# Norm factors and down-product evacuations given in parts a slot apart, and operand splits all on VectorE, in a one-layer streaming encoder

## The chip, the core and the metric

The kernel runs on one core of a Trainium2 chip. The metric is the device time of one execution in microseconds (us). TensorE (PE) multiplies matrices into PSUM, VectorE (DVE), ScalarE (ACT) and GpSimd (POOL) work element by element, and SyncE (SP) issues most of the transfers. Each engine works through its own instructions in order; an instruction that depends on another engine waits at the head of its queue, with everything behind it.

## The reference

The reference computes one inference step of a one-layer encoder for 1024 prompt frames and 8 × 16 sample frames, 1152 tokens in all. Token mixing (differential attention beside a short gated convolution) and cross-attention come first; the change touches only what follows them:

```
hf = rms_norm(x, g_ffn)
u_c, new_ffn = causal_dwconv(hf @ w_up, ffn_state, w_ffconv)   # width 3, per stream
x = x + (jax.nn.silu(u_c) * (hf @ w_gate)) @ w_down            # D_FF = 2816, D_MODEL = 1024
...
y_prompt = rms_norm(hp, g_final)
```

Everything is float32. Besides the two `y`, the keys, values and convolution states are outputs.

## The kernel before

All activations are stored transposed, model or feature index on the 128 partitions and the 1152 tokens along the row. A float32 product is made of three matmuls: each operand is split into a high part (ACT casts it, L111) and a low part (a subtraction, L112, on DVE or on POOL), and hi·hi, hi·lo and lo·hi are added up in PSUM.

The whole FFN is one function, `ffn()`, and its instructions are issued on each engine in the order in which the code is written, with no scheduler behind it. It has two stages.

**The up and gate products** are 154 *products* in the order of `seq`: for each pair of feature blocks (`s`) seven products P1 to P7 of a Winograd-style scheme on 2 × 2 blocks, where the token operands B11 to T4 are made once (`pair`, called by `tsplit`) and the weight sums S1 to S4 are made by POOL for each `s` (`ffn_sum`, L1059). A product is 24 matmuls of 288 columns (L1118). Product `n` is issued in *slot* `n`: first `read(n - 1)`, which takes the sums of the product before from PSUM (a DVE addition, L1127, or an ACT copy, L1125), then the split of the weights for product `n + 3`, then whatever the table `at[n]` holds, then the matmuls. `put(n, ...)` fills that table: the operand splits, POOL's sums, and for each pair of feature blocks `i` the convolution (`tap0` on ACT, `tap` on DVE), `silu`, `gate` and the store. Products that add to a PSUM bank whose partial sums are read on the way must come after that `read`: product 5 (P7) adds to the bank that `read(3)` reads, product 11 to the bank that `read(9)` reads, product 12 to that of `read(10)`.

For the first pair (`i` = 0) the values read from PSUM are still to be multiplied by the ratio of two norm factors (`rho`, L1132). `ones(0)` and `ones(1)` sum the squares over the partitions on PE after products 5 and 7, and `ratio1(t)`, `ratio2(t)` turn the sums of each half `t` of the tokens into the ratio: Square on ACT, two DVE operations (L1224, L1225), Ln, Exp and Square on ACT (L1226 to L1228), two DVE operations (L1234, L1235). Both halves use one scratch tile `z`.

**The down product** runs over three token ranges `c` (512, 384 and 256 columns, `LAST`). Its *steps* are for `c` = 0, 1 and for the first four output blocks of `c` = 2: one feature block times four output blocks `j`, 12 matmuls (L1399), 22 steps to a group `g`; the last four output blocks of `c` = 2 come one by one, 12 matmuls to a step, six steps to a block, the last of six matmuls. In step `i` the weights for step `i + 3` are split (`wsplit`), on four buffers, so that the ACT cast can begin when step `i - 1` has left its buffer. In the first four steps of each group the four finished output blocks of the group before are evacuated one by one: `evac` multiplies by the norm factor and adds the residual on DVE (L1359, L1360), then squares on ACT (L1363 or L226), adds the square up on POOL or DVE (L227), and multiplies by the final gain on ACT (L1366). `norm1` (L1373, step 7), `norm2` (step 9, by `rstd`, L192 to L197) and `norm3` (steps 10 to 17, L1382, and the store) finish a range.

Of the kernel before, what the change touches and what calls it, by code (L numbers as in the profile page):

```python
# [12 lines left out]
AF = mybir.ActivationFunctionType  # L13
# [4 lines left out]
D = 1024  # L18
# [33 lines left out]
class Step:  # L52
# [1008 lines left out]
    def ffn(self):  # L1061
# [97 lines left out]
        def tap0(i, m):  # L1159
            def f():  # L1160
                ss[i, m] = self.tile("xb", "xb", [T], 4)
# [26 lines left out]

        def new_u(i):
            def f():  # L1190
                for m in range(2):
# [9 lines left out]

        def tsplit(b, ks, pool=()):
            def f():
                for k in ks:
                    self.B[k][b] = self.pair("tu" if b == "T4" else "tb", "t", self.Tf[k][b], nc.gpsimd if k in pool else None,
                                             8 if b == "T4" else 24)
            return f
# [8 lines left out]

        def ratio1(t):

            def f():
                if t == 0:  # L1220
                    self.z = self.tile("tu", "z", [T])
                v, y, r = half(self.z, 0), half(self.z, 1), half(self.r, t)
                nc.scalar.activation(y, r, AF.Square)
                nc.vector.tensor_scalar(out=two(v), in0=banks(self.rps), scalar1=1.0 / D, scalar2=EPS, op0=ALU.mult, op1=ALU.add)  # L1224
                nc.vector.tensor_tensor(out=v, in0=v, in1=y, op=ALU.mult)  # L1225
                nc.scalar.activation(y, v, AF.Ln)  # L1226
                nc.scalar.activation(y, y, AF.Exp, scale=-0.5)
                nc.scalar.activation(r, y, AF.Square)  # L1228
            return f

        def ratio2(t):
            def f():
                v, y, r = half(self.z, 0), half(self.z, 1), half(self.r, t)
                nc.vector.scalar_tensor_tensor(out=v, in0=v, scalar=-0.5, in1=r, op0=ALU.mult, op1=ALU.mult)  # L1234
                nc.vector.scalar_tensor_tensor(out=r, in0=v, scalar=1.5, in1=y, op0=ALU.add, op1=ALU.mult)  # L1235
            return f
# [17 lines left out]
        put(2, tsplit("T1", (2, 3)), reopen)  # L1254
        put(3, tsplit("T3", (0, 1), (1,)))
        put(4, tsplit("T3", (2, 3), (3,)), self.tsubs[5])
        put(5, tsplit("T4", (0, 1), (1,)))
        put(6, tsplit("T4", (2, 3), (3,)))
        last = NFB // 2 - 1
        for i in range(last + 1):  # L1260
# [17 lines left out]
            else:  # L1278
                put(7, ratio1(0))
                put(8, ratio2(0), ratio1(1))  # L1280
                put(9, rho(0, 0), rho(0, 10), ratio2(1))
                put(10, rho(0, 11), rho(0, 1), streams(0, 1), tap0(0, 1))
                put(11, streams(0, 0), t1[0], tap0(0, 0))
                put(12, t1[1], t1[2], t1[3])
                put(13, silu(0, 1), t0[0], t0[1])
                put(14, t0[2], t0[3])
                put(15, silu(0, 0), gate(0, 1, 1))
                put(16, gate(0, 1, 0), store(0, 1))
                put(17, gate(0, 0, 0), gate(0, 0, 1), store(0, 0))

            for d in range(4):
                put(n + d + (1 if i else 3), sums(s + 1, d))
            if i < last:
                put(n + (3 if i else 5), load(s + 2))
                put(n + 10, load(s + 3))
                for d, m in enumerate((8, 9, 10, 13)):
                    put(n + m, sums(s + 2, d))
                put(n + 14, new_u(i + 1))

# [3 lines left out]
        steps += [(2, (j,), range(4 * u, min(4 * u + 4, NFB))) for j in range(4, KT) for u in range(6)]  # L1303
        raws, gx, graw, ys, sq = {}, {}, {}, {}, {}
        done = [0]
# [48 lines left out]

        def evac(c, j):
            a, b = LAST[c]
            n, end = b - a, b == T
            x, t = ys[c, j], self.tile("t8", "sq", [512], 2)[:, 0:n]
            nc.vector.tensor_tensor(out=t, in0=ch[c, j], in1=self.r[:, a:b], op=ALU.mult)  # L1359
            nc.vector.tensor_tensor(out=x, in0=t, in1=x, op=ALU.add)  # L1360
            if j == 0 or end and j >= KT - 2:
                sq.setdefault(c, []).append(self.tile("t8", "sum", [512], 3)[:, 0:n])
                nc.scalar.activation(sq[c][-1], x, AF.Square)  # L1363
            else:
                self.sumsq(sq[c][0], x, False, nc.vector if end else nc.gpsimd, self.tile("t8", "sq", [512], 2)[:, 0:n])
            nc.scalar.activation(x, x, AF.Identity, scale=self.g[:, 3, j:j + 1])  # L1366

# [6 lines left out]

        def norm2(c):
            a, b = LAST[c]
            y, v, r = (self.tile("t8", "nt", [512], 3)[:, 0:b - a] for _ in range(3))
            self.rstd(r, ch.pop(c), 1.0 / D, b - a, y, v)
            sq[c] = r

# [20 lines left out]

        new_u(0)()
        split(0)
# [29 lines left out]
        for i, (c, js, ks) in enumerate(steps):  # L1433
# [8 lines left out]
            if i < NFB:  # L1442
                operands(min(i + 3, NFB))
            if len(js) > 1:

                if k < 4 and i >= NFB:
                    evac(*((c, k) if g else (c - 1, 4 + k)))
                if g == 0 and c and k == 9:
                    norm2(c - 1)
                if g == 0 and c and 9 < k < 18:  # L1450
                    norm3(c - 1, k - 10)
                if 18 <= k:
                    xload(c, 4 * g + k - 18)
                if g and c < 2:
                    operands(NFB * (c + 1) + k + 1, 6)
            elif k == 8:
                xload(c, js[0])
            if len(js) == 1 and js[0] == 4 and ks[0] < 16:
                evac(c, k // 4)
            step(i)  # L1460
            if g == 0 and c and len(js) > 1 and k == 7:
                norm1(c - 1)
            if len(js) == 1 and ks[-1] == NFB - 1:
                evac(c, js[0])
            if i == NFB - 1:
                for q in range(3):
                    qload(NFB + 3 + q)
        norm1(2)
        norm2(2)
        for j in (0, 6, 1, 2, 7, 3, 4, 5):  # L1470
            norm3(2, j, *((nc.gpsimd, nc.scalar) if j > 5 else ()))
# [213 lines left out]
```

## Time and profile before

| | |
|---|---|
| median of 3 runs | 1705.56 us (1703.71 to 1707.20) |
| profiled execution | 1700.45 us, span 1698.7 us |
| PE busy | 1651.9 us (97%) |
| DVE busy | 1047.9 us (62%) |
| ACT busy | 675.9 us (40%) |
| POOL busy | 395.6 us (23%) |
| FFN products 0 to 153 | about 889 to 1396 us from the span's start |
| down product | about 1396 to 1688 us |

Times in rows are from the span's start. Busy PE counts overlapping matmuls, so a stretch can look busier than it is; the count of matmuls in a stretch, beside their pace where nothing waits, tells more.

### The profile page before, as it was taken

To read this page: it belongs to the slowest core of one execution; us is meant where nothing else is said; L and a number is where in the kernel's file an instruction comes from. 1 tells how busy PE (TensorE), PEld (TensorE's weight loads), DVE (VectorE), ACT (ScalarE), POOL (GpSimd) and SP (SyncE) were. 2 spreads that over 40 slices of the span, in tenths; PEclk is the share of its full clock that TensorE was granted. 3 is DMA by queue.
4 is the path that set the end of the run, shared out by engine and by line. 5 is a ranking of instruction groups with operands and counts; after the bars stand their busy time and mean duration, and the time that the engine had idled before them with its cause. 6 is when DMAs were issued, how large, how long until landed. Compare 5 with 4: busy or idle time off the path is not lost. (4 is left out here: it accounts for less than half of the span.)

```text
span 1698.7 us, 28128 instructions
## 1 busy us (share of the span) xinstructions
PE 1651.9 (97%) x10930; PEld 1566.5 (92%) x10930; DVE 1047.9 (62%) x1718; ACT 675.9 (40%) x1373; POOL 395.6 (23%) x425
## 2 busy tenths in 40 slices
PE   8999989999999999999998999999999999999997
PEld 7999879989999999988998999999999998889987
DVE  8757544777733343466768767767766664545565
ACT  7222543555523332254235333333333334443544
POOL 3223322111112321100344332333323311100000
PEclk9999999999999999999999999999999999999998
DMA  5756877534264433551441222222122247656663
GB/s 199 266 191 205 287 248 204 167 92 152 76 262 134 144 124 137 186 211 46 131 136 49 80 79 79 79 79 67 65 67 79 65 137 224 197 167 195 186 195 106
DMA packets 106566, 246.09 MB, mean 145 GB/s; under 512 B 18112, under 2 KB 57408, under 8 KB 106432
## 3 DMA queue, kind: packets, MB, share of 16 engines
q1 hardware_dynamic: 106144, 244.03, 44.1%
q8 instruction: 86, 1.41, 0.3%
q14 instruction: 48, 0.39, 0.1%
q10 hardware_dynamic: 288, 0.26, 0.0%
HBM read 186.86 MB, written 57.39 MB: 144 GB/s over the span
## 5 line engine op out<-in xcount | busy, mean ns | idle before, releaser
L111 ACT CAST wh<-raw 128x512 fp32r<-128x512 f32 x330 | 202.0, 617 | 352.0 <-PE ch L1399 104.4
L112 DVE TENSOR_TENSOR wl<-raw,wh 128x512 fp32r<-128x512 f32 (+1 forms) x276 | 196.3, 715 | 215.7 <-ACT wh L111 215.2
L1118 PE MATMUL ch<-t,wh 128*128 128x288 f32 x1408 | 284.4, 297 | 9.2 <-DVE xb L1127 5.3
L1118 PEld LDWEIGHTS ch<-t,wh 128*128 128x128 f32 x1408 | 227.1, 189 | 10.0 <-issue 8.8
L1118 PE MATMUL ch<-b,wh 128*128 128x288 f32 x1056 | 212.9, 296 | 0.0
L1118 PE MATMUL ch<-t,wl 128*128 128x288 f32 x704 | 207.9, 295 | 0.0
L112 POOL TENSOR_TENSOR wl<-raw,wh 128x512 fp32r<-128x512 f32 x54 | 71.2, 1320 | 450.2 <-ACT wh L111 412.9
L148 PE MATMUL mm<-xh,wh 128*128 128x384 f32 x496 | 169.7, 342 | 0.9 <-DVE t L824 0.9
L1118 PEld LDWEIGHTS ch<-b,wh 128*128 128x128 f32 x1056 | 169.4, 188 | 0.2
L150 PE MATMUL mm<-xh,wl 128*128 128x384 f32 x496 | 167.9, 338 | 0.1
L149 PE MATMUL mm<-xl,wh 128*128 128x384 f32 x496 | 167.6, 338 | 0.0
L1118 PE MATMUL ch<-b,wl 128*128 128x288 f32 x528 | 155.3, 294 | 0.0
L1399 PE MATMUL ch<-t,wh 128*128 128x512 f32 (+2 forms) x576 | 146.4, 341 | 6.0 <-ACT wh L111 5.9
L1118 PEld LDWEIGHTS ch<-t,wl 128*128 128x128 f32 x704 | 133.2, 189 | 0.0
L1399 PE MATMUL ch<-b,wh 128*128 128x512 f32 (+2 forms) x480 | 119.6, 337 | 1.2 <-ACT wh L111 1.2
L1399 PEld LDWEIGHTS ch<-t,wh 128*128 128x128 f32 x576 | 102.2, 193 | 16.1 <-ACT wh L111 7.9
L1399 PE MATMUL ch<-t,wl 128*128 128x512 f32 (+2 forms) x288 | 98.5, 342 | 1.0 <-DVE wl L112 0.7
L1118 PEld LDWEIGHTS ch<-b,wl 128*128 128x128 f32 x528 | 99.4, 188 | 0.0
L148 PEld LDWEIGHTS mm<-xh,wh 128*128 128x128 f32 x496 | 93.4, 188 | 3.7 <-issue 1.6
L150 PEld LDWEIGHTS mm<-xh,wl 128*128 128x128 f32 x496 | 93.5, 188 | 0.5 <-DVE wl L112 0.4
L149 PEld LDWEIGHTS mm<-xl,wh 128*128 128x128 f32 x496 | 93.5, 188 | 0.4
L1399 PEld LDWEIGHTS ch<-b,wh 128*128 128x128 f32 x480 | 84.3, 190 | 7.8 <-ACT wh L111 1.4
(367 smaller groups left out, 3646.7 us busy)
## 6 DMA issues: line engine op xcount, KB each, us to landing
raw<-in_w_dn SPq DMA_DIRECT2D x55, 512.0 KB, 4.0
raw<-in_w_ug SPq DMA_DIRECT2D x44, 512.0 KB, 4.7
gscr<-xb SPq DMA_DIRECT2D x22, 576.0 KB, 3.2
kv<-in_kc SPq DMA_DIRECT2D x16, 512.0 KB, 5.8
kv<-in_vc SPq DMA_DIRECT2D x16, 512.0 KB, 6.1
qd<-qscr SPq DMA_DIRECT2D x64, 128.0 KB, 3.5
kv<-in_km SPq DMA_DIRECT2D x16, 512.0 KB, 6.2
kv<-in_vm SPq DMA_DIRECT2D x16, 512.0 KB, 5.8
```

The costliest lines, as they stand in the source:

```text
L111: self.nc.scalar.copy(out=h, in_=x)
L112: (eng or self.nc.vector).tensor_tensor(out=l, in0=x, in1=fl(h), op=ALU.subtract)
L148: self.nc.tensor.matmul(out, lhsT=ah, rhs=bh, start=i == 0, stop=False)
L149: self.nc.tensor.matmul(out, lhsT=ah, rhs=bl, start=False, stop=False)
L150: self.nc.tensor.matmul(out, lhsT=al, rhs=bh, start=False, stop=i == n - 1)
L1118: nc.tensor.matmul(o, lhsT=w[:, ks], rhs=y[:, ts], start=start and k == 0 and i == 0, stop=k == 3 and i == 2, skip_group_check=True)
L1399: nc.tensor.matmul(ch[c, j], lhsT=p[:, w], rhs=y, start=k == 0 and m == 0, stop=k == NFB - 1 and m == 2)
```

## The change

Three things change, all in `ffn()`; the instructions and their sizes stay the same but for the engine of some.

1. The low parts of four operand blocks (T3 and T4, blocks 1 and 3) are subtracted on DVE, no longer on POOL.
2. The norm ratio has three parts (`ratio(t, 0..2)`), each in a later slot than the one before, and each half has its own scratch: the tile that later takes the convolution (`ss`), in place of the shared `z`. The first pair's convolution, `silu`, gates and stores move one or two slots later, and one buffer of `u` is taken a slot later for it.
3. In the down product `evac` becomes `evac1` (the two DVE operations) and `evac2` (Squares, sums and gain), which the next step calls, behind its weight split. `norm2` is spread over steps 9 and 10, `norm3` over 11 to 18. For the last range the squares of blocks 1 to 3 are added on POOL, no longer on DVE.

```diff
-            def f():
-                for k in ks:
-                    self.B[k][b] = self.pair("tu" if b == "T4" else "tb", "t", self.Tf[k][b], nc.gpsimd if k in pool else None,
+                    self.B[k][b] = self.pair("tu" if b == "T4" else "tb", "t", self.Tf[k][b], None, 8 if b == "T4" else 24)
...
+        def ratio(t, part):
...
+                if part == 0:
+                    ss[0, 1 - t] = self.tile("xb", "xb", [T], 4)
+                z = ss[0, 1 - t]
+                v, y, r = half(z, 0), half(z, 1), half(self.r, t)
+                if part == 0:
+                    nc.scalar.activation(y, r, AF.Square)
+                    nc.vector.tensor_scalar(out=two(v), in0=banks(self.rps), scalar1=1.0 / D, scalar2=EPS, op0=ALU.mult, op1=ALU.add)
+                    nc.vector.tensor_tensor(out=v, in0=v, in1=y, op=ALU.mult)
+                elif part == 1:
+                    nc.scalar.activation(y, v, AF.Ln)
+                    nc.scalar.activation(y, y, AF.Exp, scale=-0.5)
+                    nc.scalar.activation(r, y, AF.Square)
+                else:
+                    nc.vector.scalar_tensor_tensor(out=v, in0=v, scalar=-0.5, in1=r, op0=ALU.mult, op1=ALU.mult)
+                    nc.vector.scalar_tensor_tensor(out=r, in0=v, scalar=1.5, in1=y, op0=ALU.add, op1=ALU.mult)
...
-                put(9, rho(0, 0), rho(0, 10), ratio2(1))
-                put(10, rho(0, 11), rho(0, 1), streams(0, 1), tap0(0, 1))
+                put(9, ratio(0, 2), rho(0, 0), rho(0, 10), ratio(1, 1))
+                put(10, ratio(1, 2), rho(0, 11))
+                put(11, rho(0, 1), streams(0, 1), tap0(0, 1))
...
+        def evac2():
+            while part:
+                c, j = part.pop()
+                x, n, end = ys[c, j], LAST[c][1] - LAST[c][0], LAST[c][1] == T
+                if j == 0 or end and j >= KT - 2:
+                    sq.setdefault(c, []).append(self.tile("t8", "sum", [512], 3)[:, 0:n])
+                    nc.scalar.activation(sq[c][-1], x, AF.Square)
+                else:
+                    self.sumsq(sq[c][0], x, False, nc.vector if end and j > 3 else nc.gpsimd, self.tile("t8", "sq", [512], 2)[:, 0:n])
+                nc.scalar.activation(x, x, AF.Identity, scale=self.g[:, 3, j:j + 1])
...
+            evac2()
             if len(js) > 1:
 
                 if k < 4 and i >= NFB:
-                    evac(*((c, k) if g else (c - 1, 4 + k)))
-                if g == 0 and c and k == 9:
-                    norm2(c - 1)
-                if g == 0 and c and 9 < k < 18:
-                    norm3(c - 1, k - 10)
+                    evac1(*((c, k) if g else (c - 1, 4 + k)))
+                if g == 0 and c:
+                    if k in (9, 10):
+                        norm2(c - 1, k == 10)
+                    if 10 < k < 19:
+                        norm3(c - 1, k - 11)
```

PE's instructions stand in the same order before and after. Three places show what moves on the others.

DVE in slots 3 and 4, before: `u` from `ch` is a read (the first row is `read(2)`, the fourth `read(3)`), `t` from `xb` the low part of an operand block, `wl` that of a weight block.

```order
L1127 TENSOR_TENSOR u_9176<-ch_9307,u_9178 128x576
L112 TENSOR_TENSOR wl_9334<-raw_9207,wh_9333 128x512
L112 TENSOR_TENSOR t_9338<-xb_8212,t_9337 128x576
L1127 TENSOR_TENSOR u_9176<-ch_9347,u_9176 128x576
L112 TENSOR_TENSOR wl_9374<-raw_9050,wh_9373 128x512
L112 TENSOR_TENSOR t_9378<-xb_8685,t_9377 128x576
L1015 TENSOR_TENSOR xb_8923<-xb_8923,xa_8922 128x576
```

The same place after the change.

```order
L1127 TENSOR_TENSOR u_9178<-ch_9307,u_9176 128x576
L112 TENSOR_TENSOR wl_9334<-raw_9207,wh_9333 128x512
L112 TENSOR_TENSOR t_9338<-xb_8212,t_9337 128x576
L112 TENSOR_TENSOR t_9342<-xb_8447,t_9341 128x576
L1127 TENSOR_TENSOR u_9178<-ch_9347,u_9178 128x576
L112 TENSOR_TENSOR wl_9374<-raw_9050,wh_9373 128x512
L112 TENSOR_TENSOR t_9378<-xb_8685,t_9377 128x576
L112 TENSOR_TENSOR t_9382<-xb_8923,t_9381 128x576
L1015 TENSOR_TENSOR xb_8923<-xb_8923,xa_8922 128x576
```

`read(3)` has one split more in front of it, and POOL's four sums for `s` = 1, which stood in turn with these splits in POOL's queue, now stand there one after another.

ACT in slots 7 to 9, before: `z` is the ratio's scratch, `c_9_84` the norm factors, the copy into `xb_9472` is `read(8)`.

```order
L111 CAST wh_9506<-raw_9209 128x512
L1223 ACTIVATE z_9510<-c_9_84 128x576
L1226 ACTIVATE z_9510<-z_9510 128x576
L1227 ACTIVATE z_9510<-z_9510 128x576
L1228 ACTIVATE c_9_84<-z_9510 128x576
L111 CAST wh_9544<-S_1705_9345 128x512
L1223 ACTIVATE z_9510<-c_9_84 128x576
L1226 ACTIVATE z_9510<-z_9510 128x576
L1227 ACTIVATE z_9510<-z_9510 128x576
L1228 ACTIVATE c_9_84<-z_9510 128x576
L1125 COPY xb_9472<-ch_9480 128x576
L111 CAST wh_9583<-S_1734_9478 128x512
```

The same place after; `xb_9510` and `xb_9548` are the two halves' scratch.

```order
L111 CAST wh_9506<-raw_9209 128x512
L1225 ACTIVATE xb_9510<-c_9_84 128x576
L111 CAST wh_9541<-S_1705_9345 128x512
L1229 ACTIVATE xb_9510<-xb_9510 128x576
L1230 ACTIVATE xb_9510<-xb_9510 128x576
L1231 ACTIVATE c_9_84<-xb_9510 128x576
L1225 ACTIVATE xb_9548<-c_9_84 128x576
L1125 COPY xb_9472<-ch_9480 128x576
L111 CAST wh_9579<-S_1734_9478 128x512
L1229 ACTIVATE xb_9548<-xb_9548 128x576
L1230 ACTIVATE xb_9548<-xb_9548 128x576
L1231 ACTIVATE c_9_84<-xb_9548 128x576
```

`read(8)` and the weight casts have moved ahead of the Ln, Exp and Square that were given a slot earlier.

ACT at the first steps of the down product's second group for `c` = 1, before: the cast of the weights (`wh`), then Square and gain of the evacuated block (`ys`).

```order
L111 CAST wh_16133<-raw_15985 128x512
L1363 ACTIVATE sum_16142<-ys_16063 128x384
L1366 ACTIVATE ys_16063<-ys_16063,c_6_79 128x384
L111 CAST b_16145<-S_2558_15559 128x256
L111 CAST wh_16165<-raw_16023 128x512
L226 ACTIVATE sq_16172<-ys_16081 128x384
```

After.

```order
L111 CAST wh_16132<-raw_15982 128x512
L111 CAST b_16141<-S_2557_15558 128x256
L111 CAST wh_16161<-raw_16020 128x512
L1370 ACTIVATE sum_16165<-ys_16062 128x384
L1373 ACTIVATE ys_16062<-ys_16062,c_6_79 128x384
L111 CAST b_16171<-S_2562_15580 128x256
```

The next step's weight cast now stands ahead of the Square, at this and the other group changes alike.

## Rows read from the trace of the kernel before

**Rows 1.** PE's waits in the down product: total us, times, longest.

```profile
PE ch L1399 <- ACT wh L111: 7.1, 7, 1.4
```

**Rows 2.** Stretches: length, PE, PEld, DVE, ACT, POOL busy (instructions), clock, DMA.

```profile
910.00:920.00 10.00, 9.16 (x64) 8.55 (x64) 8.75 (x10) 4.08 (x7) 6.00 (x5) 1.00 0.19 56
934.20:941.00 6.80, 3.81 (x16) 3.84 (x17) 6.08 (x10) 2.65 (x4) 2.63 (x5) 0.50 0.04 5
980.00:1396.00 416.00, 416.00 (x3126) 416.00 (x3125) 288.74 (x376) 147.10 (x224) 123.61 (x161) 1.00 0.23 78
1515.00:1534.00 19.00, 17.37 (x94) 15.94 (x94) 9.41 (x15) 9.58 (x16) 5.14 (x4) 1.00 0.28 89
1565.00:1582.00 17.00, 15.76 (x89) 14.87 (x87) 9.41 (x18) 9.32 (x20) 3.03 (x3) 1.00 0.36 115
1582.00:1612.00 30.00, 30.00 (x173) 30.00 (x174) 16.80 (x34) 14.82 (x33) 0.00 (x0) 1.00 0.71 216
1612.00:1629.00 17.00, 13.11 (x96) 11.88 (x96) 8.58 (x17) 8.46 (x16) 4.02 (x4) 1.00 0.34 108
1629.00:1653.00 24.00, 24.00 (x199) 23.73 (x198) 17.40 (x31) 11.15 (x20) 0.00 (x0) 1.00 0.84 276
1653.00:1663.00 10.00, 8.30 (x61) 7.60 (x59) 5.42 (x13) 5.48 (x13) 0.00 (x0) 0.91 0.37 115
1663.00:1688.00 25.00, 25.00 (x188) 24.75 (x189) 13.45 (x26) 10.95 (x22) 0.00 (x0) 0.90 0.38 112
```

**Rows 3.** PE in order of time at products 5 and 11: start, us, instruction [idle before].

```profile
908.68 0.50 PE L1118 MATMUL ch<-t,wh 128*128 128x288 f32 x2 [3.03 <-DVE u L1127]
...
937.19 0.82 PE L1118 MATMUL ch<-t,wh 128*128 128x288 f32 x2 [5.34 <-DVE xb L1127]
```

**Rows 4.** DVE in order of time, slots 2 to 4.

```profile
902.86 1.42 DVE L112 TENSOR_TENSOR t<-xa,t 128x576 fp32r<-128x576 f32 x2
...
904.86 1.26 DVE L112 TENSOR_TENSOR wl<-raw,wh 128x512 fp32r<-128x512 f32 x1
906.04 1.82 DVE L112 TENSOR_TENSOR t<-xb,t 128x576 fp32r<-128x576 f32 x1
907.79 0.75 DVE L1127 TENSOR_TENSOR u<-ch,u 128x576 f32<-128x576 f32 x1
```

**Rows 5.** POOL in order of time: a split and a sum, and a sum of a later slot.

```profile
902.79 2.78 POOL L112 TENSOR_TENSOR t<-xb,t 128x576 fp32r<-128x576 f32 x1 [8.57 <-ACT t L111]
905.54 1.71 POOL L1059 TENSOR_TENSOR S<-raw,raw 128x512 f32<-128x512 f32 x1
...
1027.54 1.29 POOL L1059 TENSOR_TENSOR S<-raw,S 128x512 f32<-128x512 f32 x1 [2.36 <-DVE wl L112]
```

**Rows 6.** ACT in order of time, the second half's ratio and what stands behind it.

```profile
927.97 0.69 ACT L1223 ACTIVATE z<-c 128x576 f32<-128x576 f32 x1 [3.25 <-DVE c L1235]
...
931.72 0.62 ACT L1125 COPY xb<-ch 128x576 f32<-128x576 f32 x1
932.24 0.62 ACT L111 CAST wh<-S 128x512 fp32r<-128x512 f32 x1
```

**Rows 7.** ACT in order of time, first evacuation of blocks 4 to 7 of `c` = 1.

```profile
1612.90 0.62 ACT L111 CAST wh<-raw 128x512 fp32r<-128x512 f32 x1 [1.15 <-PE ch L1399]
1615.39 0.52 ACT L226 ACTIVATE sq<-ys 128x384 f32<-128x384 f32 x1 [1.88 <-DVE ys L1360]
...
1616.47 0.60 ACT L111 CAST wh<-raw 128x512 fp32r<-128x512 f32 x1
```

**Rows 8.** DVE, the same evacuation.

```profile
1613.55 0.69 DVE L112 TENSOR_TENSOR wl<-raw,wh 128x512 fp32r<-128x512 f32 x1 [1.05 <-ACT wh L111]
1614.16 0.55 DVE L1359 TENSOR_TENSOR sq<-ch,c 128x384 f32<-128x384 f32 x1
1614.74 0.56 DVE L1360 TENSOR_TENSOR ys<-sq,ys 128x384 f32<-128x384 f32 x1
```

**Rows 9.** POOL, the sum of that square.

```profile
1615.99 1.01 POOL L227 TENSOR_TENSOR sum<-sum,sq 128x384 f32<-128x384 f32 x1 [35.25 <-ACT sq L226]
```

More of the change, by code (lines that the diff above doesn't have):

```diff
@@ L1187, in store, with new_u @@
             return lambda: nc.sync.dma_start(out=self.gscr[:, 2 * i + m], in_=gs[i, m])
-        def new_u(i):
+        def new_u(i, *ms):
             def f():
-                for m in range(2):
+                for m in ms:
                     us[i, m] = self.tile("u", "u", [HALO + T], 2)
@@ L1297, in ffn @@
                     put(n + m, sums(s + 2, d))
-                put(n + 14, new_u(i + 1))
+                put(n + 14, new_u(i + 1, 1))
+                put(n + 14 + (not i), new_u(i + 1, 0))
         steps = [(c, range(4 * g, 4 * g + 4), (k,)) for c in range(3) for g in range(2) for k in range(NFB) if (c, g) != (2, 1)]
@@ L1303, in ffn @@
         steps += [(2, (j,), range(4 * u, min(4 * u + 4, NFB))) for j in range(4, KT) for u in range(6)]
-        raws, gx, graw, ys, sq = {}, {}, {}, {}, {}
+        raws, gx, graw, ys, sq, part = {}, {}, {}, {}, {}, []
         done = [0]
@@ L1353, in xload, with evac1 @@
             nc.sync.dma_start(out=ys[c, j], in_=self.x2[:, j, a:b])
-        def evac(c, j):
+        def evac1(c, j):
             a, b = LAST[c]
-            n, end = b - a, b == T
-            x, t = ys[c, j], self.tile("t8", "sq", [512], 2)[:, 0:n]
+            x, t = ys[c, j], self.tile("t8", "sq", [512], 2)[:, 0:b - a]
             nc.vector.tensor_tensor(out=t, in0=ch[c, j], in1=self.r[:, a:b], op=ALU.mult)
             nc.vector.tensor_tensor(out=x, in0=t, in1=x, op=ALU.add)
[L1361 to L1366, printed above, removed]
+            part.append((c, j))
+        def evac2():
[8 more added lines that the diff above has]
+                nc.scalar.activation(x, x, AF.Identity, scale=self.g[:, 3, j:j + 1])
         def norm1(c):
@@ L1373, in norm1, with norm2 @@
                 nc.tensor.matmul(ch[c], lhsT=self.ones, rhs=z, start=i == 0, stop=i == len(sq[c]) - 1)
-        def norm2(c):
+        def norm2(c, last=False):
             a, b = LAST[c]
-            y, v, r = (self.tile("t8", "nt", [512], 3)[:, 0:b - a] for _ in range(3))
-            self.rstd(r, ch.pop(c), 1.0 / D, b - a, y, v)
-            sq[c] = r
+            if not last:
+                y, v, r = norm = [self.tile("t8", "nt", [512], 3)[:, 0:b - a] for _ in range(3)]
+                nc.scalar.activation(y, ch[c], AF.Ln, bias=self.eps, scale=1.0 / D)
+                nc.vector.tensor_scalar(out=v, in0=ch[c], scalar1=-0.5 / D, scalar2=-0.5 * EPS, op0=ALU.mult, op1=ALU.add)
+                nc.scalar.activation(y, y, AF.Exp, scale=-0.5)
+                nc.scalar.activation(r, y, AF.Square)
+                sq[c] = norm
+            else:
+                y, v, r = sq[c]
+                nc.vector.tensor_tensor(out=v, in0=v, in1=r, op=ALU.mult)
+                nc.vector.scalar_tensor_tensor(out=r, in0=v, scalar=1.5, in1=y, op0=ALU.add, op1=ALU.mult)
+                sq[c] = r
         def norm3(c, j, eng=nc.vector, q=nc.sync):
@@ L1467, in ffn @@
                     qload(NFB + 3 + q)
+        evac2()
         norm1(2)
         norm2(2)
+        norm2(2, True)
         for j in (0, 6, 1, 2, 7, 3, 4, 5):
```

54 lines of the change are left out of this document (20 added, 34 removed).

## The prediction

> **What bounds the kernel now.** I read the chain of waits on the page first: outside PE it has hardly more than ACT and DVE work at a few places, so PE sets the time and only its holes can be won. PE's stretches come next. Between 980 and 1396 us, PE is busy throughout, 416.00 us for 3126 matmuls or 0.133 us each, so a product of 24 takes 3.19 us [rows 2]. The holes stand on either side of that stretch.
>
> At the start of the FFN, PE stands still for 3.03 us before product 5, waiting for `read(3)` on DVE, and for 5.34 us before product 11, waiting for `read(9)` [rows 3]. After the second hole began, the granted clock was 0.50 in 934.2 to 941.0, the lower of its two levels (1.2 of 2.4 GHz), while after the first it stayed at 1.00 in 910 to 920 [rows 2].
>
> In the down product I count matmuls, since busy time hides short holes. Where nothing waits, a matmul of 384 columns takes 30.00/173 = 0.173 us, one of 256 columns 24.00/199 = 0.121 us. The five disturbed stretches then lose 19 − 94 × 0.1734 = 2.7, 17 − 89 × 0.1734 = 1.6, 17 − 96 × 0.1206 = 5.4, 10 − 61 × 0.1206 = 2.6 and 25 − 188 × 0.1206 = 2.3 us, together 14.6 us; the last two are partly the clock, at 0.91 and 0.90 [rows 2]. PE waits there for the weight cast on ACT, seven times, 7.1 us by its records [rows 1].
>
> **The down product, part by part.** In the evacuation steps before, ACT casts the weights at 1612.90, then stands with Square at its head until DVE has subtracted, multiplied and added, and starts Square at 1615.39; the next cast starts at 1616.47 [rows 7]. So one step lasts 1616.47 − 1612.90 = 3.57 us, though PE needs 12 × 0.121 = 1.45. DVE's share is 0.69 + 0.55 + 0.56 = 1.80 us [rows 8], ACT's own 0.62 + 0.52 and a gain that ends by the next cast (16.47 − 15.39 = 1.08 for Square and gain), 1.7 in all. Neither engine is full; the chain that runs from one to the other and back is. Four such steps fall behind by 4 × (3.57 − 1.45) = 8.5 us, and the lead of three steps (4.3 us) covers half; 4.2 of the 5.4 us are explained so.
>
> With `evac2` a step later the next cast stands ahead of Square, and DVE works on the next weights while ACT squares. A step then costs the busier engine, DVE, 1.8 us, and up to 1.0 more where POOL's sum (1.01 us [rows 9]) takes turns with it. The lag is 4 × (1.8 − 1.45) = 1.4 us, at worst 4 × (2.8 − 1.45) = 5.4. I take 1.8 with two such turns in four steps, 1.4 + 2.0 = 3.4 us, inside the lead of 4.3: no hole. For `c` = 1 the step is 12 × 0.173 = 2.08 us and the same work falls behind less; at the single blocks of `c` = 2 all operations are shorter (256 columns). The sums moved from DVE to POOL there end long before the last block, whose tail is unchanged. `norm2` in two parts and `norm3` a step later add no instruction; DVE has 0.69 + 0.56 in a 1.45 us step there, and `norm1` is in time as long as the last of four sums ends two steps after the last evacuation. SP's stores move by one step behind one more weight load, which nothing waits for. Of the 14.6 us I keep 0.4 as a rest: gain 14.2. With no hole there is nothing that I can see to drop the clock near 1661 us, so its share is in that sum.
>
> **The start of the FFN.** Three effects, in order of the slots.
>
> *Splits on DVE.* Four low parts leave POOL. Beside POOL, a DVE split took 1.82 us at 906.04 and a weight split 1.26 at 904.86, against 0.71 each for the two at 902.86, while the read at 907.79, one of whose inputs is PSUM, took its plain 0.75 [rows 4]. POOL's sum took 1.71 at 905.54 and 1.29 at 1027.54; its split of 902.79 took 2.78, about as long as the two DVE splits beside it and then itself [rows 5]. The DVE split is longer by 1.1, most of one POOL operation: the two take turns, whole instruction by whole instruction. Each added split costs DVE 0.7 and saves such a turn, about zero for DVE as a whole. But the sums of `s` = 1, so far held behind POOL's splits, now come one after another from about 902.9 on, when DVE has read the old S3. Before `read(3)`, DVE has a weight split and two operand splits, three turns at 1.29.
>
> Walk: `read(2)` ends at 904.9; without POOL, 0.6 + 2 × 0.7 bring `read(3)` to an end at 907.6. With three turns, one begun during `read(2)`, it ends at 910.5 and product 5 starts at 910.6, 1.9 us later than before. I take the turns, because the rows at 904.86 and 906.04 show one in front of each.
>
> The Trainium skill, "SBUF — State Buffer", section "Who interferes with whom", says that a DVE instruction with two SBUF inputs and a GpSimd instruction that reads SBUF exclude each other, the later one blocked to the end of the first. By that rule the four sums, now in one run, give back at the start what moving the splits saves, and the time is the one forecast here; if DVE went first, as it did at 902.86, it would be that of the first rival. The rows at 904.86 and 906.04 agree with the rule, those of 1.26 and 1.82 us against 0.71.
>
> *The clock.* Product 4 ends at 908.68 − 3.03 = 905.65, so the hole becomes 4.95 us. A hole of 5.34 us brought the clock down in this trace and one of 3.03 did not; at 4.95 I expect a fall, of the same 6.8 us at half speed, so 3.4 us lost.
>
> *The ratio.* Before, the second half's first Square waited 3.25 us for the end of the first half's ratio (the shared `z`), and `read(8)` and the next weight cast started only at 931.72 and 932.24 behind its Ln, Exp and Square [rows 6]; the ratio's end on DVE and then `read(9)`, for which PE waited, came after both. Now `read(8)` and the cast stand ahead of them, and `read(9)` stands behind the cast's low part, the first half's two last operations and two `rho`, while the second half's end comes after it.
>
> From 910.6, product 11 can start on PE after six products, two `ones` of about 0.8 and the clock loss: 910.6 + 19.2 + 1.6 + 3.4 = 934.8. On the other side, product 8 ends at 928.4, ACT copies and casts to 929.6, DVE takes one turn (1.3), the low part, four operations of 0.7 and `read(9)`, ending at about 934.8. They meet; product 11 starts at 935, product 12 at 938.1 at full clock. Before, product 11 started at 937.19 and lost 3.81/2 = 1.9 us to the half clock [rows 2], so product 12 followed at 942.3. Gain 4.2 us.
>
> The bounds: if POOL takes no turns, the hole before product 5 is 2.0 us, there is no fall, and product 11 starts when DVE is through, about 932: gain 7.2. On the other side, products 11, 12 and 17 are each met with under 0.5 us to spare by this walk, and one more turn for each costs 3 × 1.29 = 3.9: gain 0.3. The convolution, `silu` and gates, one or two slots later, come into slots where DVE has 2 to 3 us of work for 3.19 and hide there; their stores end before the buffers are taken again three slots later. If that cover were gone, one turn (1.3 us) would show.
>
> **Sum.** 14.2 + 4.2 = 18.4 us off the profiled execution, 1700.45 − 18.4 = 1682.0. That execution stood 5.1 us under the median of runs; from the median, 1705.56 − 18.4 = 1687.2.
>
> **Rivals.**
>
> *No fall of the clock* (24 in 100). For it: 3.03 us left the clock alone, and POOL may get fewer turns, as at 902.86. Against it: the turns at 904.86 and 906.04. Gain 7.2 + 14.2 = 21.4, time 1684.2.
>
> *The sums hold Square* (18). ACT's Square and DVE's product share two `sq` buffers, so a Square must wait until POOL has added the one before. A step is then 0.52 + 1.01 + a turn of up to 0.7 = 2.2 us, four fall behind by 3.1, and with the 1.4 us that a weight split takes the lead is used up; in the second half of the down product (5.4 + 2.6 + 2.3) about half stays. Against it: POOL's sum can run while DVE reads PSUM. Gain 4.2 + 14.2 − 5.2, time 1692.4.
>
> *No difference* (4). The stalls only change their names, ACT behind DVE becoming DVE behind ACT, and the start gives back 3: about 1705.
>
> *Slower* (4). POOL in front of DVE. If all seven sums of the first two sets take a turn before `read(9)`, DVE has 7 × 1.29 + 4 × 0.7 = 11.8 us more in front of it; product 5 starts at 912, 3.3 us later than before, the clock falls there (3.4 us) and again at product 11, which waits as before, and products 12 and 17 wait a turn each (2.6): 9.3 us lost. This decides once `read(9)` ends after about 940, and it makes the kernel slower only if POOL's turns also keep two thirds of the holes in the down product: +9.3 − 4.9, time 1710.
>
> My own case has 50 in 100. About 0.2%, 3.4 us, is what a measurement of this kernel tells from none: faster 0.92, same 0.04, slower 0.04. The range reaches from the second case less the noise of the runs to beyond the third, 1680 to 1697.
>
> **What would show it.** Right: in the down product no wait of PE for the weight cast near the four group changes, 0.121 us a matmul through them, Square about one step behind its addition, clock 1.00 up to the tail; at the start a hole of 4 to 5 us at product 5 ended by `read(3)`, a half-clock stretch right after it, POOL's four sums in one run beside DVE splits of 1.8 us, and no hole at product 11. Wrong: a hole before product 11 or 12 of over 1.5 us, PE waiting for a cast that waited for a Square behind POOL's sum, or the clock at half near the end of the down product without a hole.

## The result and the profile after

The changed kernel takes 1679.64 us (median of 4 runs, 1678.54 to 1682.56) where the kernel before, timed beside it, takes 1704.63 (1703.46 to 1707.20, 4 runs): a ratio of 0.9854, interval 0.9836 to 0.9872. It is faster by 25 us, not by the 18.4 forecast, and ends 0.36 us below the stated range. The profiled execution took 1678.54 us, span 1676.8, granted clock 0.994 on average. Its page begins so (share of the span, instructions):

```profile
PE 1642.3 (98%) x10930; PEld 1562.9 (93%) x10930; DVE 1052.8 (63%) x1719; ACT 677.7 (40%) x1373; POOL 390.9 (23%) x424
```

I cut each execution at three marks: the first matmul of product 0, the first of the down product, and the end of its last one.

| us from the span's start | before | after |
|---|---|---|
| product 0 begins | 889.50 | 888.94 |
| down product begins | 1396.01 | 1389.77 |
| its last matmul ends | 1687.93 | 1666.07 |
| span | 1698.7 | 1676.8 |
| products 0 to 153 | 506.51 | 500.83 |
| down product | 291.92 | 276.30 |

Between the two profiles, 5.68 us come from the start of the FFN, 15.62 from the down product and 0.56 from ahead of product 0, where nothing is changed. The tail behind the last matmul is 10.7 us in both.

**Down product.** PE's waits from product 0 on, by what it waited for (total us, times, longest). The first belongs to the start. In the down product the seven for the weight cast [rows 1] are gone; the norm's sum (L1380) is left.

```profile
PE ch L1118 <- DVE u L1127: 4.6, 1, 4.6
...
PE ch L1380 <- ACT sum L1370: 0.6, 1, 0.6
```

Stretches after, in the columns of [rows 2]. The first belongs to the start and is read below; the second is the undisturbed middle of the FFN, the others span disturbed parts of the down product.

```profile
909.80:913.20 3.40, 3.40 (x15) 3.40 (x16) 3.40 (x6) 0.00 (x0) 0.23 (x1) 0.50 0.44 116
970.00:1386.00 416.00, 416.00 (x3126) 416.00 (x3125) 288.72 (x374) 148.04 (x226) 125.81 (x164) 1.00 0.23 77
1505.00:1524.00 19.00, 19.00 (x105) 18.22 (x104) 13.60 (x19) 10.47 (x18) 5.19 (x4) 1.00 0.47 156
1602.00:1619.00 17.00, 17.00 (x141) 16.73 (x140) 12.92 (x21) 12.60 (x23) 4.07 (x4) 1.00 0.58 180
1619.00:1643.00 24.00, 24.00 (x203) 24.00 (x202) 18.75 (x35) 12.69 (x25) 2.08 (x3) 1.00 0.82 258
1643.00:1653.00 10.00, 10.00 (x86) 10.00 (x85) 6.96 (x14) 5.72 (x12) 0.15 (x1) 1.00 0.74 208
1653.00:1666.00 13.00, 13.00 (x110) 13.00 (x110) 5.67 (x11) 5.32 (x11) 0.00 (x0) 1.00 0.18 55
```

The middle is the same, 3126 matmuls in 416 us. Below it the count is the thing to read: 105 in 19 us where there were 94, and 141 in 17, 203 in 24, 86 in 10 and 110 in 13 us, 0.116 to 0.121 us each, where [rows 2] had 96 in 17 and 61 in 10.

PE's order is the same in both kernels, so each matmul can also be set beside itself. Counted from the first matmul of the stage, the kernel before falls behind by 2.6, 2.0, 5.5 and 5.6 us at the four group changes: the matmul that starts at 1628.53 before, behind the third, starts at 1612.23 after, 232.52 us into its stage against 222.46. The last of the four holds the 6.8 us at half clock from 1661.2 of the kernel before, worth at most 3.4 us; after the change the clock stays at 1.00 there.

ACT in the evacuation that answers to [rows 7]:

```profile
1603.43 0.62 ACT L111 CAST wh<-raw 128x512 fp32r<-128x512 f32 x1 [0.86 <-PE ch L1416]
1604.45 0.52 ACT L226 ACTIVATE sq<-ys 128x384 f32<-128x384 f32 x1 [0.40 <-DVE ys L1361]
1605.01 0.62 ACT L1373 ACTIVATE ys<-ys,c 128x384 f32<-128x384 f32 x1
1605.53 0.60 ACT L111 CAST wh<-raw 128x512 fp32r<-128x512 f32 x1
1606.58 0.53 ACT L226 ACTIVATE sq<-ys 128x384 f32<-128x384 f32 x1 [0.45 <-DVE ys L1361]
```

From cast to cast it is 1605.53 − 1603.43 = 2.10 us, before 3.57. Square still starts right behind its own addition (1603.80 + 0.56 = 1604.36, Square at 1604.45) and waits 0.40 us for it. But the block it squares is that of the step before the cast at 1603.43, so no chain runs any more from one cast through DVE's addition and Square to the next cast, and DVE goes from one step to the next without a pause. Its addition takes 0.56 us in the first step, as in [rows 8], and 1.02 in the next, where POOL's sum runs beside it from 1605.05 and lasts as long: the two take turns (DVE's rows, then POOL's).

```profile
1603.80 0.56 DVE L1361 TENSOR_TENSOR ys<-sq,ys 128x384 f32<-128x384 f32 x1
1604.27 0.69 DVE L112 TENSOR_TENSOR wl<-raw,wh 128x512 fp32r<-128x512 f32 x1
1604.88 0.55 DVE L1360 TENSOR_TENSOR sq<-ch,c 128x384 f32<-128x384 f32 x1
1605.46 1.02 DVE L1361 TENSOR_TENSOR ys<-sq,ys 128x384 f32<-128x384 f32 x1
1606.41 0.68 DVE L112 TENSOR_TENSOR wl<-raw,wh 128x512 fp32r<-128x512 f32 x1
...
1636.83 0.43 DVE L1361 TENSOR_TENSOR ys<-sq,ys 128x256 f32<-128x256 f32 x1 [0.84 <-DMA ys<-x]
```

```profile
1605.05 1.02 POOL L227 TENSOR_TENSOR sum<-sum,sq 128x384 f32<-128x384 f32 x1 [38.01 <-ACT sq L226]
```

Four such steps fall behind by 4 × (2.10 − 1.45) = 2.6 us, inside the lead of 4.3. DVE also waits for the residual's transfer now (0.84 us at 1636.83), which PE does not feel.

**Start of the FFN.** PE's answer to [rows 3], then DVE and POOL in the place of [rows 4, 5].

```profile
909.72 0.75 PE L1118 MATMUL ch<-t,wh 128*128 128x288 f32 x2 [4.63 <-DVE u L1127]
```

```profile
904.31 1.12 DVE L112 TENSOR_TENSOR wl<-raw,wh 128x512 fp32r<-128x512 f32 x1
905.35 3.55 DVE L112 TENSOR_TENSOR t<-xb,t 128x576 fp32r<-128x576 f32 x2
908.83 0.74 DVE L1127 TENSOR_TENSOR u<-ch,u 128x576 f32<-128x576 f32 x1
...
931.45 0.75 DVE L1127 TENSOR_TENSOR xb<-ch,xb 128x576 f32<-128x576 f32 x1
```

```profile
902.47 2.41 POOL L1059 TENSOR_TENSOR S<-raw,raw 128x512 f32<-128x512 f32 x1 [7.83 <-DVE wl L112]
904.96 1.60 POOL L1059 TENSOR_TENSOR raw<-raw 128x512 f32<-128x512 f32 x1
906.63 1.66 POOL L1059 TENSOR_TENSOR S<-raw,raw 128x512 f32<-128x512 f32 x1
908.37 1.66 POOL L1059 TENSOR_TENSOR S<-raw,S 128x512 f32<-128x512 f32 x1
```

POOL's four sums stand in one run; beside them two DVE splits take 3.55 us (1.42 where DVE had the way, [rows 4]), `read(3)` ends at 909.6, and the hole before product 5 grows from 3.03 to 4.63 us. The clock falls in the stretch from 909.80, but that lasts 3.40 us. After it PE shows no wait: `read(9)` is through at 932.2, product 11 starts at 932.39 with no hole before it, and product 12 at 935.86. ACT has `read(8)` and the weight cast ahead of the ratio's second part, where they stood behind it until 931.72 [rows 6]:

```profile
926.19 0.64 ACT L1125 COPY xb<-ch 128x576 f32<-128x576 f32 x1 [1.07 <-PE ch L1118]
926.73 0.62 ACT L111 CAST wh<-S 128x512 fp32r<-128x512 f32 x1
927.25 0.69 ACT L1229 ACTIVATE xb<-xb 128x576 f32<-128x576 f32 x1
```

### The profile page after: what moved, and what is told of

Its sections match the earlier page's. It is cut to its first block, busy times and chain, and to the rows that moved or that the text cites. A ratio compares the mean times of both kernels' runs of the same rounds, so it can differ in the third digit from the quotient of the medians.

```text
span 1676.8 us, 28132 instructions
## 1 busy us (share of the span) xinstructions
PE 1642.3 (98%) x10930; PEld 1562.9 (93%) x10930; DVE 1052.8 (63%) x1719; ACT 677.7 (40%) x1373; POOL 390.9 (23%) x424
## 4 chain that ended last, share of the span: by engine, by line
PE 88%; DVE 6%; ACT 3%; DMA 2%; issue 1%; POOL 0%; DVEq 0%; SPq 0%; ACTq 0%; POOLq 0%
PE ch L1118 29%; PE ch L1416 16%; PE mm L148 8%; PE mm L150 8%; PE mm L149 8%; PE tr L148 3%; PE tr L149 3%; PE tr L150 3%; PE tr L655 2%; PE sc L616 1%; PE tr L642 1%; PE sc L523 0%; DVE t L112 0%; PE mm L817 0%; DVE p L631 0%
## 5 line engine op out<-in xcount | busy, mean ns | idle before, releaser
L1118 PEld LDWEIGHTS ch<-b,wh 128*128 128x128 f32 x1056 | 169.4, 188 | 0.5 <-issue 0.3
L1059 POOL TENSOR_TENSOR S<-raw,raw 128x512 f32<-128x512 f32 x44 | 73.5, 1670 | 81.0 <-DVE wl L112 78.4
```

Of the source, the lines that this page charges most:

```text
L1059: self.nc.gpsimd.tensor_tensor(out=w[o], in0=w[x], in1=w[y], op=op)
L1118: nc.tensor.matmul(o, lhsT=w[:, ks], rhs=y[:, ts], start=start and k == 0 and i == 0, stop=k == 3 and i == 2, skip_group_check=True)
```

## The experiments

The theory: the down product's gain comes from `evac2` running a step later, the start's gain from the ratio given in parts, and the splits on DVE are worth about nothing, since they trade POOL's splits for POOL's sums in the turns. Rivals: that the splits carry part of the gain; that the last range's sums on POOL or the spread norm, not the step later, mend the evacuation; that the whole difference includes a drift of the runs. A kernel's ratio below is to the kernel before in the same session, the stages are those of the table.

| | ratio (interval) | products 0–153 | down product |
|---|---|---|---|
| down part alone | 0.9905 (0.9892–0.9918) | 506.68 | 276.30 |
| start alone | 0.9979 (0.9970–0.9988) | 500.84 | 294.03 |
| `evac2` in the same step | 0.9977 (0.9968–0.9987) | 500.66 | 293.89 |
| before, itself | 1.0001 (0.9991–1.0012) | 506.75 | 292.08 |
| splits alone | 1.0004 (0.9995–1.0013) | 508.69 | 292.10 |
| ratio alone | 0.9969 (0.9956–0.9981) | 500.24 | 293.89 |
| sums of `s` = 1 on DVE | 0.9866 (0.9851–0.9880) | 498.71 | 276.30 |
| after, itself | 0.9880 (0.9864–0.9895) | 500.84 | 276.30 |
| all but the splits | 0.9866 (0.9831–0.9901) | 500.22 | 276.30 |
| `read(3)` first | 0.9860 (0.9831–0.9889) | 499.14 | 276.30 |

### The two halves apart

The kernel before with the down product's hunks of the change alone, and with the hunks of the start alone:

```diff
+            evac2()
             if len(js) > 1:
...
-                    evac(*((c, k) if g else (c - 1, 4 + k)))
+                    evac1(*((c, k) if g else (c - 1, 4 + k)))
```

> Only the down product's part of the change (evacuation in two parts a step apart, the last norm in parts). Theory A, the two halves of the change are independent and each hole is the chain between ACT and DVE: the down product takes 276.3 us from its first to its last matmul as in the changed kernel (291.9 before), the FFN products keep their 506.5 us; time about 1704.6 - 15.6 = 1689, or down to 1685 if other executions lose more to the clock than the profiled one. Rival, the down product's gain came from the clock or the transfers being moved by the earlier part: less than 10 us of gain here.

> Only the FFN's start (operand splits on DVE, norm ratio in three parts, convolution one or two slots later). Theory A: the FFN products take 500.8 us (506.5 before), the down product keeps 291.9; time about 1704.6 - 5.7 = 1699, or 1697 if one more fall of the clock goes. Rival, the parts depend on each other: the gains of this and of the down product alone do not add up to the 25.0 us between the medians by more than 4 us.

The down part alone takes 1686.38 us beside 1702.17 and has the down product of the changed kernel to the hundredth, 276.30. Its PE waits at the FFN's start are the old ones:

```profile
PE ch L1118 <- DVE xb L1127: 5.3, 1, 5.3
PE ch L1118 <- DVE u L1127: 3.0, 1, 3.0
```

The start alone takes 1698.88, with the products' 500.84. So each part alone gives its own stage the changed kernel's time. The test of the expectation, whole gains that add up to 25.0 us within 4, is missed all the same: 15.8 + 3.3 = 19.1. The 25.0 was itself high, a later session has 19.9 for the changed kernel; and the start alone loses some of its gain again, since its down product, whose code is that of before, takes 294.03 instead of 291.92. The waits are the same seven of 7.1 us; what differs is the clock. Here is the start alone in two stretches of the down product:

```profile
1620.30:1627.10 6.80, 5.70 (x22) 4.58 (x21) 3.22 (x6) 3.83 (x7) 0.99 (x1) 0.50 0.45 136
1657.90:1664.70 6.80, 6.32 (x29) 5.79 (x28) 4.54 (x9) 4.06 (x9) 0.00 (x0) 0.50 0.31 83
```

Of the six profiles that have the holes, three had one such fall (1661.2 in the kernel before) and three had two; the six without the holes had none. All three with two have the ratio in parts, and so reach the down product some 6 us sooner; why that matters stays open. The price is the 2 us by which the stage differs.

### The evacuation in one step

The changed kernel, with `evac2` called where `evac1` ends:

```diff
             part.append((c, j))
+            evac2()
```

> The changed kernel with one thing put back: the second part of each evacuation (Square, sum, gain) is called in the same step as the first, ahead of the next weight cast. Theory A, the order of cast and Square on ACT makes the holes: they come back at the four group changes, a step of 4.05 us at 512 columns and 3.56 at 384, down product about 290 us, time about 1679.6 + 14 = 1694 or more. Rival B, the move of the last sums from DVE to POOL and of the norm's parts made the gain: holes stay away at the first three changes and the time stays within 4 us of 1679.6.

The old holes are back, 6.8 us in seven waits, and the down product takes 293.89. ACT stands with Square at the head of its queue for 2.15 us, and 4.05 us lie from cast to cast:

```profile
1520.00 0.61 ACT L111 CAST wh<-raw 128x512 fp32r<-128x512 f32 x1
1522.76 0.63 ACT L226 ACTIVATE sq<-ys 128x512 f32<-128x512 f32 x1 [2.15 <-DVE ys L1361]
1523.42 0.73 ACT L1374 ACTIVATE ys<-ys,c 128x512 f32<-128x512 f32 x1
1524.05 0.60 ACT L111 CAST wh<-raw 128x512 fp32r<-128x512 f32 x1
```

The time is 1698.99 us (about 290 and 1694 were expected). This kernel has the sums on POOL, the spread norm and everything else of the change, and by themselves they gain nothing in the down product: without the step later nothing is left of its gain. That the stage is 2 us longer than before goes with a second fall of the clock, near 1621, as in the start alone. Whether the step later would do as well without the spread norm was not run.

### The kernel before, against itself

> The kernel before itself, for the spread of its executions: the profiled one took 1700.5 us where the runs took 1703.5 to 1707.2. Theory C, the difference is the clock, each hole lets it fall in some executions and not in others: executions of about 1704 show a mean granted clock below the 0.991 of the profiled one, by about 3 to 4 us / 1700 times two, so 0.986 to 0.988, and a profile has one more half-clock stretch. Rival, the difference has nothing to do with the clock: the granted clock is 0.991 in the longer executions too.

It came out at 1702.68 (1699.43 to 1706.57, 12 runs), ratio 1.0001; its profiled run took 1704.06, its clock 0.989, where 0.986 to 0.988 was expected; over the twelve runs the clock goes from 0.992 in the shortest to 0.988 and 0.989 in the two longest. The stages from product 0 on repeat to 0.2 us, but product 0 begins at 892.69, 3.2 us later than in the profile that the prediction went by. Over all profiles it begins between 888.94 and 893.15, whatever the kernel. One place where this arises is near 40 us: this profile of the kernel before, and then the one that the prediction went by.

```profile
40.20:47.00 6.80, 6.63 (x18) 5.54 (x19) 5.87 (x12) 1.66 (x4) 3.32 (x5) 0.50 0.55 163
```

```profile
40.20:47.00 6.80, 6.80 (x39) 6.30 (x38) 6.54 (x13) 1.67 (x4) 4.04 (x5) 1.00 0.60 183
```

It has 18 matmuls in the stretch against 39: the clock is at its lower level in one execution of the same code and not in the other. The kernel before has medians of 1704.63, 1702.17, 1701.98 and 1702.17 in the four sessions, the three later ones each on another chip, so the 1705.56 of three runs lay about 3 us above what it usually takes.

### The start, taken apart

The four splits on DVE and nothing else; and the ratio in parts with its moved slots and nothing else:

```diff
-        put(3, tsplit("T3", (0, 1), (1,)))
+        put(3, tsplit("T3", (0, 1)))
...
```

```diff
...
-                put(8, ratio2(0), ratio1(1))
-                put(9, rho(0, 0), rho(0, 10), ratio2(1))
+                put(8, ratio(0, 1), ratio(1, 0))
+                put(9, ratio(0, 2), rho(0, 0), rho(0, 10), ratio(1, 1))
...
```

> Only the four operand splits moved from POOL to DVE, all else as before. Theory D, the splits give nothing by themselves, since POOL's sums then run beside DVE in one go: product 5 waits 4.6 us and the clock falls as in the changed kernel, product 11 still waits over 4 us; FFN products 506.5 to 509 us, time within 3 us of the kernel before. Rival, taking POOL off DVE's port is itself the gain: the hole before product 11 shrinks by more than 2 us and the FFN products take under 504.5 us.

> Only the norm ratio in three parts with two scratch tiles and the convolution later; the four splits stay on POOL. Theory D, this part makes the whole gain at the start: hole of 3.0 us before product 5 without a fall of the clock, no hole over 1 us before product 11, FFN products 499 to 501 us. Rival, the ratio needs DVE free of POOL's splits: a hole of over 2 us stays before product 11 and the FFN products take more than 502.5 us.

The splits alone make the products 2.2 us longer (508.69 against 506.51): the hole at product 5 grows to 4.63 us, the clock falls there, and product 11 still waits.

```profile
913.87 0.82 PE L1118 MATMUL ch<-t,wh 128*128 128x288 f32 x2 [4.63 <-DVE u L1127]
...
942.71 0.82 PE L1118 MATMUL ch<-t,wh 128*128 128x288 f32 x2 [4.87 <-DVE xb L1127]
```

In the whole time that does not show (1.0004). The ratio alone gives the start's gain in full, 500.24. It keeps the hole of 3.04 us before product 5:

```profile
909.39 0.50 PE L1118 MATMUL ch<-t,wh 128*128 128x288 f32 x2 [3.04 <-DVE u L1127]
```

Yet the clock fell for 3.40 us from 910.2 in this one, behind a hole no longer than that of [rows 3], behind which it had not fallen; no fall was expected here.

### POOL's sums taken out of the way

The changed kernel with the sums of `s` = 1 on DVE:

```diff
-        self.nc.gpsimd.tensor_tensor(out=w[o], in0=w[x], in1=w[y], op=op)
+        (self.nc.vector if s == 1 else self.nc.gpsimd).tensor_tensor(out=w[o], in0=w[x], in1=w[y], op=op)
```

> The changed kernel with the four weight sums of s = 1 on DVE too, so that POOL is idle in slots 3 to 6. Theory E, a POOL sum beside DVE costs DVE a turn of up to 1.3 us and on DVE 0.6: read(3) ends by 907.8 (in the changed kernel's time), the hole before product 5 shrinks to 2 to 3 us and the clock doesn't fall, but product 11 is bound by DVE, so the FFN products gain 0.3 to 2 us of 500.8 only. Rival 1, the hole before product 5 is itself the price: they gain 3.5 us or more. Rival 2, DVE and POOL share the port by turns of less than an instruction and POOL's help was real: read(3) ends no earlier and the products take 1 us or more longer.

> The changed kernel itself beside the kernel before on one chip. Theory C, the spread of both kernels lies in the first 50 us, which the change doesn't touch: its executions spread over about 4 us, the longer ones with a half-clock stretch near 40 us and the first FFN product 2 to 3 us later; the FFN products take 500.8 and the down product 276.3 us whatever the total is; ratio to the kernel before 0.986 to 0.988. Rival, the spread belongs to the FFN's holes: the stages from product 0 on vary by 2 us or more from one profile to the other.

DVE now carries four additions more and is through earlier all the same, since the splits are back at 1.42 us a pair:

```profile
906.53 0.68 DVE L112 TENSOR_TENSOR wl<-raw,wh 128x512 fp32r<-128x512 f32 x1
907.13 1.42 DVE L112 TENSOR_TENSOR t<-xb,t 128x576 fp32r<-128x576 f32 x2
908.47 0.69 DVE L1059 TENSOR_TENSOR S<-raw,raw 128x512 f32<-128x512 f32 x1
909.07 0.75 DVE L1127 TENSOR_TENSOR u<-ch,u 128x576 f32<-128x576 f32 x1
```

Product 0 begins at 891.16 in this trace and at 888.94 in that of the changed kernel; counted from there, `read(3)` ends 18.66 us on against 20.63, 2.0 us earlier. The hole before product 5 is 2.65 us, the products take 498.71, 2.1 less than the changed kernel's 500.84 beside it. So the turns are real and worth about 2 us. The Trainium skill, "SBUF — State Buffer", section "Who interferes with whom", has a DVE instruction with two SBUF inputs and a GpSimd one that reads SBUF exclude each other to the end of the first; 3.55 us beside the sums against 1.42 without them agree. The clock fell all the same, for 3.40 us at 909.4, so the shorter hole did not save it, against the expectation. The changed kernel itself repeats its stages, 500.84 and 276.30, and begins product 0 at 892.42, 3.5 us later than in its first profile. In whole times the two cannot be told apart well: 1678.56 (1677.64 to 1683.03) and 1682.04 (1679.40 to 1685.33), the intervals of the ratios overlapping.

### Without the splits, and with the read first

The changed kernel with the four splits back on POOL; and the kernel with the sums of `s` = 1 on DVE, but with `read(3)` ahead of the later splits and of the sums:

```diff
...
-        put(3, tsplit("T3", (0, 1)))
+        put(3, tsplit("T3", (0, 1), (1,)))
...
```

```diff
...
-                put(n + d + (1 if i else 3), sums(s + 1, d))
+                put(n + d + 1 if i else (4, 5, 5, 8)[d], sums(s + 1, d))
...
+            if n == 3:
+                pass
+            elif n == 4:
+                tsplit("T3", (2, 3))()
+                split(6)
+                split(7)
...
```

> The changed kernel with the four operand splits back on POOL; ratio and down product as changed. Theory D, the splits on DVE are no gain in this change: FFN products 500.2 us as with the ratio alone (500.8 in the changed kernel), hole of 3.0 us before product 5, down product 276.3; time the same as the changed kernel within 2 us, 0.6 us less by the stages. Rival, the parts only work together: the products take over 502.5 us, or the down product over 278.

> The changed kernel with the four weight sums of s = 1 on DVE (as in the run with the sums on DVE) and, in slots 3 and 4, read(3) and the T3 splits ahead of the weight splits 6 and 7 and of the first sum. Theory F, DVE's queue in front of read(3) is all that holds product 5, so read(3) ends 1.2 us earlier by the two instructions of 0.6 us that now stand behind it: hole before product 5 of 1.3 to 1.6 us (2.65 with the sums alone), no fall of the clock there (worth 1.7 us), and FFN products 495.5 to 497.5 us (498.7 with the sums alone); time 1.5 to 3 us under that. Rival, DVE's work as a whole up to read(9) sets product 11: a hole of 1 to 3 us opens before product 11 or 12 and the products stay within 0.7 us of 498.7.

Without the splits the products take 500.22, 0.6 us less than with them, and no fall of the clock follows product 5. That is as much as the ratio alone (500.24), which has the same code in this stage and had the fall: here PE gets ahead and waits for operand splits instead:

```profile
912.33 0.50 PE L1118 MATMUL ch<-t,wh 128*128 128x288 f32 x2 [3.04 <-DVE u L1127]
915.15 0.40 PE L1118 MATMUL ch<-t,wh 128*128 128x288 f32 x1 [0.86 <-DVE t L112]
923.80 0.40 PE L1118 MATMUL ch<-t,wh 128*128 128x288 f32 x1 [1.04 <-DVE t L112]
```

So with the splits on POOL DVE sets the pace that far, and the fall cost nothing.

With the read first, the hole before product 5 is 1.45 us, and there is no fall either. But three new holes appear, and the products take 499.14, where 495.5 to 497.5 was expected, not less than with the sums on DVE alone:

```profile
909.00 0.50 PE L1118 MATMUL ch<-t,wh 128*128 128x288 f32 x2 [1.45 <-DVE u L1127]
917.41 0.50 PE L1118 MATMUL ch<-t,wh 128*128 128x288 f32 x2 [0.82 <-ACT wh L111]
921.41 1.21 PE L1215 MATMUL ch<-acc,c 128*128 128x288 f32 x4 [0.31 <-DVE xb L1226]
933.10 0.50 PE L1118 MATMUL ch<-t,wh 128*128 128x288 f32 x2 [0.90 <-DVE xb L1127]
```

What is saved at product 5 is given back by product 11, where `read(9)` ends last: all DVE's work up to there has to be done, in whatever order.

## Why the prediction was right and wrong

**Right: the mechanism of the down product.** All holes that wait for the cast are gone, at the price that was given for a step: DVE's 1.8 us plus turns with POOL made 2.10, and the loop from Square back to the next cast is cut. One sign did not come: Square was to start about one step behind its addition and starts 0.1 us behind it, waiting for DVE as before; what counts is that the Square ahead of a cast is now that of the step before. The experiment with one step shows that nothing else of the change did it.

**The size was low by 1.4 us** (15.6 measured, 14.2 forecast). The rest of 0.4 that I kept was not there, and the five stretches, counted by matmuls, gave 2.7, 1.6, 5.4 and 2.6 + 2.3 us, 14.6 in all, where the matmuls set beside themselves lag by 2.6, 2.0, 5.5 and 5.6. Part of the other 1.0 is the pace that I counted by: 24.00/199 came from a stretch that I took for full. It holds the norm's two slow matmuls at 1629.83 (0.81 us together), and after the change 203 matmuls fit into as long a stretch without them. The difference of a whole stage, from first to last matmul, would have been the better measure of what a stage without holes can give.

**Right: the walk at the start as far as product 5.** The hole was to be 4.95 us and was 4.63, ended by `read(3)`, with POOL's four sums in one run. The splits were forecast at about zero for DVE; they are a loss of 0.6 us with the ratio and 2.2 without it, so the ratio's parts give the whole gain of the start.

**Wrong: the clock's fall**, the term "of the same 6.8 us at half speed, so 3.4 us lost". It came where it was expected and lasted 3.40 us, so it cost PE at most 1.7. In the eleven falls at products 5 and 11 in all profiles, PE was at work at most 0.6 us after the fall began where it lasted 3.4 us (six, among them 909.80 and 909.72 here), and 0.9 us or more after where it lasted 6.8 (five, among them 934.2 and 937.19 before). That is a pattern, not a cause shown. Also, I let a fall hang on the length of the hole, 3.03 no and 4.95 yes; holes of 2.65 and 3.04 us had one in these runs, one of 1.45 had none, and 3.04 without the splits had none.

The DVE side of product 11 carried the same term, since it was walked from the end of product 8 (928.4), behind the fall: `read(8)` started at 926.19, and `read(9)` ended at 932.2, not 934.8. The two sides do meet, as forecast, PE starting product 11 at 932.39, but 2.6 us earlier; of these about 1.7 are the clock, 0.56 the earlier start of product 0 in this profile and 0.3 the shorter hole. Product 12 came at 935.86, not 938.1, and the start gave 5.7 us, not 4.2.

**Wrong: the base that the sum was taken from**, the larger part of the miss. The sum was worked out on a profile of 1700.45 us and moved unchanged to a median of three runs, 1705.56. I noted the 5.1 us between them and made no allowance for them. The four sessions give the kernel before 1702 to 1704.6. Of the 7.5 us by which 1705.56 − 18.4 was too high, 2.9 are the two terms above (21.3 measured in the stages, 18.4 forecast), 0.9 the base itself (1704.63 with a fourth run), and 3.7 what the medians differ by beyond the stages (25.0 − 21.3); with the right terms the sum would still have read 1684.3. Taken from 1702.17, the forecast sum gives 1683.8; the measured 21.3 us of both stages give 1680.9, where the later sessions have 1678.6 to 1682.0 for the changed kernel and its near variants. In the first session the medians are 25.0 us apart and the profiles 21.9; in the later one with the changed kernel itself it is 1701.98 − 1682.04 = 19.9. The stages do not differ by that much (500.83 and 500.84, 276.30 twice); the start of product 0 does, so I put the 3.7 us down to the chance of these executions: no run shows the change at work there.

**Rivals.** The sums do not hold Square back: no wait of PE for a cast is left. POOL in front of DVE is a real effect of the stated kind, one turn at each split, but stays at 2 us, far from the point at which it decides. The rival with no fall of the clock (1684.2) missed the mechanism at product 5; that its gain of 21.4 is nearly the 21.3 that came is luck.

## What to carry to other kernels

Where two in-order engines hand one block back and forth and each also feeds the matrix engine, put the second engine's half one step later, behind its feeding work: 3.6 us a step became 2.1 with not one instruction less. Measure what a stage could give between its own first and last matmul, in two executions, before summing holes, and compare stages with stages, or, where PE's order is the same, each matmul with itself: stages repeated to 0.2 us here while whole times spread over 4 to 7. An operation taken off a slow engine is worth only what it delays there; here it let other work of that engine collide with the same reader, and moving that other work too brought more.

## What the runs showed of the hardware that was not expected

- Half-clock stretches ahead of the tail lasted 3.4 or 6.8 us in every trace. The same hole of 4.63 us before product 5 was followed by 3.4 us of it in four profiles with the splits on DVE and by 6.8 in a fifth; two executions of the changed kernel had 3.4 and 6.8 us of it near 9 us, and only one of them had it near 40.
- Moving four additions from POOL to DVE (0.69 us each there, 1.6 to 2.4 on POOL) made DVE ready earlier by 2 us: two operand splits beside them fell from 3.55 to 1.42 us.
- In the down product, holes of at most 1.4 us with PE otherwise busy were followed by a fall of the clock between 1657 and 1668 us in all six profiles that had the holes, and near 1621 in three of them; the six without the holes had none.
